# A decode step of a hybrid decoder: the read matrix of the sample state filled by four strided copies in place of sixteen small ones

## Chip, cores and metric

The kernel runs on one core of one Trainium2 chip. The metric is the device time of one launch in microseconds (us), as the median of several runs. What is timed is one inference step for two groups of tokens that share all weights: a prompt of 512 tokens, and a sample group of 8 batches with 4 new tokens each (32 tokens). The kernel holds them side by side as 544 columns; columns 512 to 543 are the sample tokens.

## What is computed

Two layers, each a mixer, a cross-attention into 256 memory tokens, and a feed-forward layer. The mixer of layer 0 joins Mamba-2 state-space heads with sliding-window attention. The change lies in the state-space part of the sample group. For each of 8 batches there is a state of 16 heads by 64 by 128, and the reference does this for the batch's 4 tokens:

```python
def ssd_chunk(h, inp, a_neg):
    x, dt, bm, cm = inp
    rep = SSM_HEADS // SSM_GROUPS
    bh = jnp.repeat(bm, rep, axis=2)
    ch = jnp.repeat(cm, rep, axis=2)
    cs = jnp.cumsum(dt * a_neg, axis=1)
    ...
    scores = jnp.einsum('bthn,bshn->btsh', ch, bh) * decay
    y = jnp.einsum('btsh,bshp->bthp', scores, xdt)
    y = y + jnp.einsum('bthn,bhpn->bthp', ch, h) * jnp.exp(cs)[..., None]
    w_end = jnp.exp(cs[:, -1:, :] - cs)
    h_new = h * jnp.exp(cs[:, -1, :])[:, :, None, None] + jnp.einsum('bsh,bshn,bshp->bhpn', w_end, bh, xdt)
    return h_new, y
```

The matrix that the change fills holds `cm` (C), for the product of C with the old state `h`. There are two groups of 8 heads, each with its own C of 4 columns a batch.

## The kernel before

Nearly all time is matmuls on TensorE (PE), whose 32-bit weights and activations are split into a high and a low part: `wpiece` loads a piece of weights into `room` by the SP queue (L165), ScalarE (ACT) casts the high part (L169) and VectorE (DVE) subtracts to get the low one (L170, tile `split_t`). `mm` (L138) records all matmuls.

The stage around the change is `even`, layer 0. A string of letters there says in which order four generators are advanced: `s` state-space work of the prompt (`ssm`), `p` that of the samples (`ssm_sample`), `f` filler matmuls (the first half of the output projection `wo_e`, then the cross-attention's memory keys and values, `mem_k` and `mem_v`), and `g` the gates with the sum of squares of a norm (`gates`, `norm_tile`, `rstd`). After them comes the second half of `wo_e` (tiles `xh`, `xl`, evacuated by `ssm_evac`). The letters set only where the code stands: the program is built with a scheduler that plays the code through with its own estimates of time and lays down the order of each engine's instructions from that. A small edit can so move instructions of other code.

In `ssm_sample` the tile `CmYi` holds two things. `Cm`, its first 512 columns, is C spread out: for group g and batch b a block of 32 columns in which only columns 4b to 4b+3 are filled, the rest zero (the clear at L971). The 16 copies at L976 on GpSimd (POOL) fill them. A batch's state is loaded into `hb` by SP (L994), two batches to a tile; PE multiplies with `Cm` (matmuls of `hb,CmYi`, all into one PSUM tile, `pi`, here ps_587), POOL decays the state (L1005), PE forms the update from `X4` and `Bm`, DVE adds it (L1006), SP stores it (L1007). When `pi` has its sum over all 8 batches, DVE scales it into `Yi`, the other part of `CmYi` (L1011, one for each group). PE then runs a stretch of small matmuls, here called the small group: 8 of `room,CmYi` (128x32) and 16 of `sE,sxdt` (32x32), into ps_632. DVE adds the result to `xs` (L1019), multiplies by the gates (L913), and forms the parts of the norm's input (`split`, L259).

`mem_v` ends with two evacuations by DVE (L1407, from ps_620 and ps_621). The norm's sum of squares is gathered on POOL (L268), PE adds it over the partitions (`rstd`: ps_645, ps_654), DVE scales it (L302), POOL takes the power (L303), and PE spreads the result over all partitions (ps_646), from where DVE copies it (L310).

Of the kernel before, what the change touches and what calls it, by code (L numbers as in the profile page):

```python
# [106 lines left out]
class Net:  # L107
# [808 lines left out]
    def ssm_sample(self, xs, BC, dt, dtA, sm):  # L916
        B = lambda g: BC[:, g]
        C = lambda g: BC[:, 2 + g]
        nc, I, O = self.nc, self.I, self.O
# [6 lines left out]
        cy = self.H("CmYi")  # L926
        Cm = cy[:, 0:512].rearrange("p (g b t) -> p g b t", g=2, b=8)
# [43 lines left out]
        nc.gpsimd.memset(Cm, 0.0)  # L971
        for g in range(2):
            nc.gpsimd.memset(Yi[64 - 64 * g:128 - 64 * g, 8 * g:8 * g + 8], 0.0)
        for g in range(2):
            for b in range(8):
                nc.gpsimd.tensor_copy(Cm[:, g, b, 4 * b:4 * b + 4], C(g)[:, 512 + 4 * b:516 + 4 * b])  # L976
        yield
        R = sm.tile([32, 16, 32], F32, tag="t2E", bufs=3, name=self.nm("sR"))
        nc.vector.tensor_tensor(R, Ub.unsqueeze(1).to_broadcast([32, 16, 32]), dA.unsqueeze(2).to_broadcast([32, 16, 32]), ALU.mult)
# [37 lines left out]
        for j in range(8):  # L1017
            x = xs[j][:, tok]
# [903 lines left out]
```

## Time and profile before

| what | value |
|---|---|
| median of 3 runs | 1657.58 us (1655.66 to 1658.09) |
| the profiled execution | 1655.56 us |
| its span, first to last instruction | 1653.8 us |
| PE busy | 1623.4 us, 98% of the span |
| DVE, ACT, POOL busy | 1195.5, 795.2, 310.6 us |
| PE's share of the chain that ended last | 73% |
| mean granted TensorE clock | 0.993 of full speed |

The span is the time between the first and the last instruction that the profiler recorded; 1.76 us of the profiled execution lie around it. An engine's busy time is the sum of its instructions. The granted clock is what the chip allowed TensorE: 1.00 is 2.4 GHz, 0.50 is 1.2 GHz, and a value between is a mean over a stretch with both. In a timeline, a row's columns are the start, the time to the end of its last instruction, the engine, line, operation, output from inputs with shape, how many alike stand in the row, and in brackets the idle time of the engine before it with what ended that.

### The profile page before, as it was taken

How to read it: one execution, taken by the hardware profiler on the slowest of the kernel's cores; microseconds unless marked ns; L12 is line 12 of the kernel's file. 1: busy time of each engine (PE TensorE's matmuls, PEld its weight loads, DVE VectorE, ACT ScalarE, POOL GpSimd, SP SyncE). 2: the span in 40 equal slices, each digit the busy share in tenths (PEclk: the TensorE clock that was granted, in tenths of full speed). 3: DMA queues.
4: the chain of work that ended last, by engine and by line, in shares of the span. 5: the costliest groups of instructions: out<-in, count | busy, mean ns of one | idle time of the engine just before them, and what ended most of it. 6: DMA issues, size and time to landing. Idle time of an engine off the chain costs nothing.

```text
span 1653.8 us, 32422 instructions
## 1 busy us (share of the span) xinstructions
PE 1623.4 (98%) x12720; PEld 1518.6 (92%) x12720; DVE 1195.5 (72%) x2327; ACT 795.2 (48%) x1629; POOL 310.6 (19%) x482
## 2 busy tenths in 40 slices
PE   8999999999999999999999999998999999999998
PEld 7999999878998999999999996656989999999997
DVE  6788789888777877777767478546567986767754
ACT  5467545444445444444435266435445444444434
POOL 0022333763322300000002113111313200000002
PEclk9999999999999999999999999999999999999999
DMA  5221334138342232323213433555441322323222
GB/s 194 65 65 52 123 111 161 40 128 290 119 170 73 66 133 87 106 81 111 86 69 138 143 112 119 173 170 178 147 179 54 122 101 77 115 84 103 77 74 84
DMA packets 71221, 189.27 MB, mean 114 GB/s; under 512 B 7612, under 2 KB 34012, under 8 KB 63452
## 3 DMA queue, kind: packets, MB, share of 16 engines
q1 hardware_dynamic: 69932, 185.43, 33.8%
q8 instruction: 100, 1.64, 0.4%
q10 hardware_dynamic: 1056, 1.24, 0.3%
q0 software_dynamic: 80, 0.52, 0.1%
q14 instruction: 53, 0.43, 0.1%
HBM read 172.22 MB, written 14.95 MB: 113 GB/s over the span
## 4 chain that ended last, share of the span: by engine, by line
PE 73%; DVE 2%; ACT 1%; issue 1%; DMA 0%; POOL 0%; POOLq 0%; DVEq 0%; SPq 0%; ACTq 0%
PE ps L138 48%; PE ps L1632 23%; PE ps L141 2%; DMA fr<-wfi 0%; DVE split_t L170 0%; DVE xn L1573 0%; POOL prt L1210 0%; ACT prt L1198 0%; DVE prt L1197 0%; ACT prt L1321 0%; DVE xf L1568 0%; DVE PT L1180 0%; DVE xpr L1473 0%; ACT split_t L169 0%; ACT PT L1180 0%
## 5 line engine op out<-in xcount | busy, mean ns | idle before, releaser
L138 PE MATMUL ps<-xh,split_t 128*128 128x288 f32 (+1 forms) x2304 | 463.2, 293 | 8.2 <-ACT split_t L169 7.8
L138 PEld LDWEIGHTS ps<-xh,split_t 128*128 128x128 f32 x2304 | 371.0, 190 | 11.2 <-ACT split_t L169 7.8
L1632 PE MATMUL ps<-xf,split_t 128*128 128x272 f32 x2592 | 350.5, 289 | 0.2 <-ACT split_t L1605 0.2
L138 PE MATMUL ps<-xl,split_t 128*128 128x256 f32 (+1 forms) x1152 | 337.9, 294 | 0.0
L1632 PEld LDWEIGHTS ps<-xf,split_t 128*128 128x128 f32 x2592 | 335.7, 188 | 1.1 <-DVE split_t L1606 0.8
L268 POOL TENSOR_TENSOR room<-room,sq 128x256 f32<-128x256 f32 (+1 forms) x96 | 84.8, 888 | 782.4 <-ACT sq L267 781.0
L138 PEld LDWEIGHTS ps<-xl,split_t 128*128 128x128 f32 x1152 | 218.6, 190 | 1.1 <-issue 0.4
L138 PE MATMUL ps<-hh,fs 128*128 128x256 f32 (+1 forms) x1024 | 208.3, 288 | 0.0
L169 ACT CAST split_t<-room 128x1024 fp32r<-128x1024 f32 (+1 forms) x128 | 130.3, 1019 | 136.3 <-PE ps L138 108.3
L170 DVE TENSOR_TENSOR split_t<-room,split_t 128x1024 fp32r<-128x1024 f32 (+1 forms) x128 | 163.8, 1282 | 26.9 <-ACT split_t L169 26.1
L1605 ACT CAST split_t<-fr 128x1024 fp32r<-128x1024 f32 x108 | 113.6, 1052 | 113.2 <-PE ps L1632 49.4
L138 PEld LDWEIGHTS ps<-hh,fs 128*128 128x128 f32 x1024 | 165.7, 188 | 0.0
L1606 DVE TENSOR_TENSOR split_t<-fr,split_t 128x1024 fp32r<-128x1024 f32 x108 | 133.0, 1231 | 42.7 <-ACT split_t L1605 40.0
L138 PE MATMUL ps<-hl,fs 128*128 128x256 f32 (+1 forms) x512 | 147.2, 288 | 0.0
L138 PE MATMUL ps<-oh,split_t 128*128 128x288 f32 (+1 forms) x512 | 102.0, 294 | 0.0
L138 PEld LDWEIGHTS ps<-hl,fs 128*128 128x128 f32 x512 | 96.4, 188 | 0.0
L138 PEld LDWEIGHTS ps<-oh,split_t 128*128 128x128 f32 x512 | 81.6, 190 | 1.8 <-issue 1.8
L138 PE MATMUL ps<-ol,split_t 128*128 128x288 f32 (+1 forms) x256 | 75.3, 295 | 0.0
L138 PE MATMUL ps<-hh,split_t 128*128 128x256 f32 (+1 forms) x384 | 73.5, 289 | 0.0
L1606 DVE TENSOR_TENSOR fs<-fr,fs 128x512 fp32r<-128x512 f32 x36 | 24.9, 691 | 65.1 <-ACT fs L1605 65.1
L258 ACT ACTIVATE xh<-x,room 128x256 fp32r<-128x256 f32 (+1 forms) x96 | 48.1, 517 | 48.9 <-DVE x L323 28.6
L1677 ACT CAST fs<-room 128x512 fp32r<-128x512 f32 x64 | 39.7, 620 | 65.0 <-PE ps L138 56.1
(428 smaller groups left out, 3150.2 us busy)
## 6 DMA issues: line engine op xcount, KB each, us to landing
fr<-wfi SPq DMA_DIRECT2D x36, 1024.0 KB
room<-wfo SPq DMA_DIRECT2D x64, 256.0 KB
room<-wo_e SPq DMA_DIRECT2D x16, 512.0 KB
xk<-mem_k SPq DMA_DIRECT2D x8, 1024.0 KB
xv<-mem_v SPq DMA_DIRECT2D x8, 1024.0 KB
room<-wfi SPq DMA_DIRECT2D x16, 512.0 KB
fox_k<-fox_k SPq DMA_DIRECT2D x64, 128.0 KB
fox_v<-fox_v SPq DMA_DIRECT2D x64, 128.0 KB
```

The lines of the kernel that those rows point to most:

```text
L138: return self.placed(self.nc.tensor.matmul(out, lhsT, rhs, start=start, stop=stop))
L141: return self.placed(self.nc.tensor.transpose(out, in_, self.ident[0:k, 0:k]))
L169: nc.scalar.copy(hi[:, 0:n], raw[:, 0:n])
L170: nc.vector.tensor_tensor(lo[:, 0:n], raw[:, 0:n], hi[:, 0:n].bitcast(F32), ALU.subtract)
L258: nc.scalar.activation(hh, src, AF.Copy, scale=g)
L268: nc.gpsimd.tensor_tensor(acc, acc, sq[:, 0:N], ALU.add)
L1605: nc.scalar.copy(hi, t)
L1606: nc.vector.tensor_tensor(lo, t, hi.bitcast(F32), ALU.subtract)
L1632: self.nc.tensor.matmul(ps, w[a][:, k], x[:, b, k], start=start and k == 0 and i == 0, stop=k == 3 and i == 2, skip_group_check=True)
L1677: nc.scalar.copy(hi, raw)
```

## The change

The 16 copies of 4 columns each become 4: for each group one copy of the first seven batches, as 7 blocks of 4 columns that lie 36 apart in `Cm` (L977), and one of the last batch (L978). The same values land in the same places, and the clears stay.

```diff
         for g in range(2):
             nc.gpsimd.memset(Yi[64 - 64 * g:128 - 64 * g, 8 * g:8 * g + 8], 0.0)
+
         for g in range(2):
-            for b in range(8):
-                nc.gpsimd.tensor_copy(Cm[:, g, b, 4 * b:4 * b + 4], C(g)[:, 512 + 4 * b:516 + 4 * b])
+            step = cy[:, 256 * g:256 * g + 252].rearrange("p (b x) -> p b x", x=36)
+            nc.gpsimd.tensor_copy(step[:, :, 0:4], C(g)[:, 512:540].rearrange("p (b t) -> p b t", t=4))
+            nc.gpsimd.tensor_copy(Cm[:, g, 7, 28:32], C(g)[:, 540:544])
```

Lines behind the edit are higher by 2: L1005, L1006, L1011, L1019 and L1407 become L1007, L1008, L1013, L1021 and L1409. No other line of code differs. The scheduler's order does: of PE's 12,087 instructions those from about the 2550th to the 3010th stand in another order, which is the stretch from 343 to 430 us, and the same stretch differs on DVE, ACT, POOL and SP. Ahead of it and behind it the order is the same. In the rows below the first number of a name is the tile's, the second only counts buffers and is lower by 12 in the changed program.

On DVE at the end of `mem_v` the order was, before (`mkv` is what L1407 writes; `CmYi` from `ps_587` is L1011):

```order
L170 TENSOR_TENSOR split_t_68<-room_67,split_t_68 128x1024
L1011 TENSOR_TENSOR CmYi_578_4312<-ps_587_4412,secs_4311 64x512 x2
L1006 TENSOR_TENSOR hb_615_4769<-hb_615_4769,ps_623_4836 128x512
L1006 TENSOR_TENSOR hb_615_4769<-hb_615_4769,ps_624_4840 128x512
L170 TENSOR_TENSOR split_t_68<-room_67,split_t_68 128x1024
L1407 TENSOR_SCALAR mkv_606_4648<-ps_620_4814,room_67 128x512
L259 SCALAR_TENSOR_TENSOR xl_635_4960<-xs_431_2982,room_67,xh_634_4959 128x256 x4
L1407 TENSOR_SCALAR mkv_606_4648<-ps_621_4815,room_67 128x512
```

and is now:

```order
L1008 TENSOR_TENSOR hb_615_4757<-hb_615_4757,ps_618_4767 128x512
L1409 TENSOR_SCALAR mkv_606_4636<-ps_620_4802,room_67 128x512
L170 TENSOR_TENSOR split_t_68<-room_67,split_t_68 128x1024
L1409 TENSOR_SCALAR mkv_606_4636<-ps_621_4803,room_67 128x512
L1013 TENSOR_TENSOR CmYi_578_4312<-ps_587_4400,secs_4311 64x512 x2
L1008 TENSOR_TENSOR hb_615_4757<-hb_615_4757,ps_623_4824 128x512
```

Two evacuations of `mem_v` and a split of weights, which stood behind the two instructions that write `Yi`, stand ahead of them.

On PE, at the same place, the last matmuls of `mem_v` (into ps_620 and ps_621) and what follows up to the small group (`ps_632`) are now:

```order
L138 MATMUL ps_620_4802<-split_t_68,memh_607_4638 128x512
L138 MATMUL ps_621_4803<-split_t_68,memh_607_4638 128x512
L138 MATMUL ps_621_4803<-split_t_68,meml_608_4639 128x512
L138 MATMUL ps_621_4803<-split_t_68,memh_607_4638 128x512
L138 MATMUL ps_587_4400<-hb_625_4863,CmYi_578_4312 32x512 x2
L138 MATMUL ps_623_4824<-X4_4322,Bm_622_4822 128x512
L138 MATMUL ps_624_4828<-X4_4322,Bm_622_4822 128x512
L138 MATMUL ps_660_5079<-xh_634_4947,split_t_68 128x256
L138 MATMUL ps_664_5112<-xh_634_4947,split_t_68 128x256
L138 MATMUL ps_632_4912<-room_67,CmYi_578_4312 128x32
L138 MATMUL ps_632_4912<-sE_586_4396,sxdt_4323 64x32 x2
```

Before, the last four `hb,CmYi` matmuls stood ahead of 24 matmuls of `mem_v` and two of `X4,Bm`, and the small group came behind those; now the last two of them close `mem_v`, with four matmuls between them and the small group.

On DVE at the norm, the rows from the gates to the scaling of the sum (`col` from `ps_645`) were, before:

```order
L259 SCALAR_TENSOR_TENSOR xl_635_4960<-xs_431_2982,room_67,xh_634_4959 128x288 x3
L302 TENSOR_SCALAR col_633_4957<-ps_645_5008 128x2
L259 SCALAR_TENSOR_TENSOR xl_635_4960<-xs_431_2982,room_67,xh_634_4959 128x288
L259 SCALAR_TENSOR_TENSOR xl_640_4984<-xs_448_3259,room_67,xh_639_4983 128x288 x4
L310 COPY room_67<-ps_646_5013 128x256
```

and are now:

```order
L259 SCALAR_TENSOR_TENSOR xl_635_4948<-xs_431_2982,room_67,xh_634_4947 128x288 x3
L259 SCALAR_TENSOR_TENSOR xl_640_4972<-xs_448_3259,room_67,xh_639_4971 128x288 x4
L1008 TENSOR_TENSOR hb_625_4863<-hb_625_4863,ps_631_4905 128x512
L302 TENSOR_SCALAR col_633_4945<-ps_645_4996 128x2
L310 COPY room_67<-ps_646_5001 128x256
```

The scaling has moved behind all eight parts of the norm's input and an update of the state. On PE its reader, ps_646, stood between two `xh` matmuls of the sixth of eight tiles of ps_670; it now stands behind all of ps_670, with the three `128x1` matmuls of ps_654 next. On POOL the seventh L268, for which ps_654 waits, stands behind L303.

## Rows read from the trace of the kernel before

**Rows 1.** The page's busy time by engine, with share of the span and instructions.

```profile
PE 1623.4 (98%) x12720; PEld 1518.6 (92%) x12720; DVE 1195.5 (72%) x2327; ACT 795.2 (48%) x1629; POOL 310.6 (19%) x482
```

**Rows 2.** Instructions on `CmYi`: ns least/median/most, first to last start in us.

```profile
L138 PE MATMUL ps<-hb,CmYi x32: 592/605/617, 360.9 to 390.0; 128*32 128x512 f32 x32
L976 POOL COPY CmYi<-BC x16: 176/178/1176, 336.7 to 345.3; 128x4 f32<-128x4 f32 x16
```

**Rows 3.** Timeline of POOL, 335 to 342 us: around the first nine copies.

```profile
335.49 1.27 POOL L873 TENSOR_TENSOR E<-E,CBm 128x512 f32<-128x512 f32 x1
336.71 0.30 POOL L976 COPY CmYi<-BC 128x4 f32<-128x4 f32 x2
...
340.45 1.90 POOL L976 COPY CmYi<-BC 128x4 f32<-128x4 f32 x7
```

**Rows 4.** Timeline of DVE at the same place.

```profile
336.28 5.30 DVE L170 TENSOR_TENSOR split_t<-room,split_t 128x1024 fp32r<-128x1024 f32 x1 [0.41 <-ACT split_t L169]
```

**Rows 5.** Timeline of PE at the same place.

```profile
342.68 0.66 PE L138 MATMUL ps<-cs,ohs 128*128 128x128 f32 x4 [1.34 <-DVE E L870]
```

**Rows 6.** Stretches: us, busy PE, PEld, DVE, ACT, POOL (instructions), granted clock, DMA share, GB/s.

```profile
345.00:350.00 5.00, 5.00 (x25) 4.43 (x25) 2.22 (x5) 0.29 (x1) 4.33 (x7) 0.68 0.00 0
396.00:400.00 4.00, 4.00 (x32) 3.20 (x30) 3.93 (x8) 2.65 (x5) 0.00 (x0) 0.93 0.69 237
400.00:404.00 4.00, 4.00 (x25) 3.62 (x26) 3.80 (x12) 1.04 (x1) 0.00 (x0) 0.50 0.78 270
404.00:408.00 4.00, 4.00 (x26) 3.96 (x26) 2.88 (x8) 0.13 (x1) 0.00 (x0) 0.72 0.99 354
414.00:420.00 6.00, 5.96 (x44) 5.69 (x45) 5.91 (x10) 1.77 (x4) 4.48 (x5) 1.00 0.65 259
```

**Rows 7.** Timeline of PE, 389 to 403 us: last `hb,CmYi`, end of `mem_v`, small group.

```profile
389.52 1.06 PE L138 MATMUL ps<-hb,CmYi 128*32 128x512 f32 x8
...
396.32 0.39 PE L138 MATMUL ps<-split_t,memh 128*128 128x512 f32 x1
396.55 0.30 PE L138 MATMUL ps<-room,CmYi 128*128 128x32 f32 x2
...
402.94 0.56 PE L138 MATMUL ps<-xh,split_t 128*128 128x256 f32 x1
```

**Rows 8.** Timeline of DVE, 385 to 402 us.

```profile
386.65 1.96 DVE L170 TENSOR_TENSOR split_t<-room,split_t 128x1024 fp32r<-128x1024 f32 x1 [0.67 <-ACT split_t L169]
...
390.76 1.40 DVE L1011 TENSOR_TENSOR CmYi<-ps,secs 64x512 f32<-64x512 f32 x2
...
394.71 1.23 DVE L170 TENSOR_TENSOR split_t<-room,split_t 128x1024 fp32r<-128x1024 f32 x1
396.07 0.75 DVE L1407 TENSOR_SCALAR mkv<-ps,room 128x512 f32<-128x512 f32 x1
...
401.10 0.68 DVE L1006 TENSOR_TENSOR hb<-hb,ps 128x512 f32<-128x512 f32 x1
```

**Rows 9.** Timeline of DVE at the norm, 414 to 418 us.

```profile
414.02 0.16 DVE L302 TENSOR_SCALAR col<-ps 128x2 f32<-128x2 f32 x1 [0.45 <-PE ps L138]
414.09 3.33 DVE L259 SCALAR_TENSOR_TENSOR xl<-xs,room,xh 128x288 fp32r<-128x288 f32 x5
```

**Rows 10.** Timeline of POOL at the norm.

```profile
414.26 0.91 POOL L303 TENSOR_TENSOR col<-col,room 128x2 f32<-128x2 f32 x1 [1.44 <-DVE col L302]
415.14 3.83 POOL L268 TENSOR_TENSOR room<-room,sq 128x288 f32<-128x288 f32 x4
```

**Rows 11.** Timeline of PE at the norm.

```profile
416.05 0.60 PE L138 MATMUL ps<-room,col 128*128 128x128 f32 x4
...
417.48 0.40 PE L138 MATMUL ps<-xl,split_t 128*128 128x288 f32 x1
```

**Rows 12.** Timeline of the SP queue, 376 to 384 us: the issues of loads.

```profile
377.16 0.81 SPq L994 DMA_DIRECT2D hb<-state  x2
...
382.38 0.33 SPq L165 DMA_DIRECT2D room<-wxv  x1
```

## The prediction

> **What bounds the kernel now.** I first read the busy time by engine: PE works 98% of the span [rows 1], so the kernel's time is PE's matmuls plus whatever keeps PE idle or slow. POOL, whose instructions the change cuts, has 19%. A POOL copy can cost time only through who waits for it. So the second view is that of the instructions on `CmYi`: the 16 copies lie between 336.7 and 345.3 us, and the first matmul that reads them starts at 360.9 us [rows 2], over 15 us later. Nobody waits for them. Third come the timelines of POOL, DVE and PE around them [rows 3 to 5], for a hidden cost; there is one, below. Since the scheduler also moved other instructions, the fourth step is the stretch from 389 to 420 us, where the new order differs in ways that PE can feel: stretches [rows 6] and the timelines of PE, DVE and POOL [rows 7 to 11]. The reader is to see there that PE never waits, but that DVE is nearly full (5.91 of 6 us from 414 to 420 us), so what DVE does first decides what PE gets in time.
>
> **The copies themselves: 0.** The sixteen take 16 x 0.18 = 2.9 us at their median, one of them 1.18 [rows 2]. The four new ones were never measured; the bounds are 4 x 0.18 = 0.7 us, if a copy's price hardly depends on its columns, and the old 2.9, if it goes by columns. I take the lower, since the old copies of 4 columns are all fixed cost. The 2 us that POOL saves are covered by the 15 us up to the first reader; were that cover gone, at most 2.2 us of gain would show.
>
> Behind them lies the hidden cost. DVE's L170 at 336.28 us lasts 5.30 us [rows 4], against 1.23 for the same operation at 394.71 [rows 8]. During it POOL works without a break, L873 and copies among it [rows 3], and PE then idles 1.34 us for DVE [rows 5]; shortly after, the clock averages 0.68 over 5 us, a loss of 0.32 x 5 = 1.6 us [rows 6]. But L170 gets through only at the seven copies of 340.45, behind L873, two copies and three more operations of POOL. In the new order the same five operations with the first two new copies stand ahead of that point, so I let the stall stay. By the Trainium skill (SBUF — State Buffer, Who interferes with whom) a DVE instruction with two SBUF inputs and a GpSimd one that reads SBUF contend for one port pair, an exclusive lock that goes to whoever starts first, while the other fully blocks. By that rule L170, waiting since 336.28, should have had the pair when the next POOL instruction ended; the trace agrees with the blocking but has it wait through several of them, and I go by the trace.
>
> **A: a new wait ahead of the small group, +2.1.** Before, `Yi` was written at 390.76 to 392.2 us and the small group that reads it began at 396.55: over 4 us of slack [rows 7, 8]. Now DVE first evacuates ps_620, splits a piece of weights, and evacuates ps_621. Count from the end of the last ps_620 matmul. PE still has three ps_621 matmuls at 0.23 (the step from 396.32 to 396.55), two of `hb,CmYi` (four took 1.0, so 0.5), two `X4,Bm` of the same 512 columns (0.46), and two of 256 columns (0.23): 1.9 us [rows 7]. DVE has 0.75 + 1.23 + 0.75 and the first of two L1013 at 0.70, 3.4 us, or 3.3 with their small overlaps [rows 8]. Least wait: 1.4 us. The split can be held up as at 386.65, where it took 1.96 while POOL ran L1005 [rows 8]: +0.7; the same L1007 of the last state pairs runs here, so I take 2.1. If DVE comes late by an L1008 (0.68) and part of a further split ahead, it is 3.5. Queued behind `Yi` on DVE are the state updates, `xl` parts and L1021; those wait for the small group or have readers after it.
>
> **B: a new wait at the norm, +0.7.** Before, L302 stood amid the L259 parts, POOL's L303 followed at 414.26, and ps_646 ran at 416.05 unwaited, 0.9 us after L303's end [rows 9 to 11]. Now behind the last L259 come L1008 (0.68, about 0.61 to the next start), L302 with 0.24 to L303's start, and L303 (0.91): 1.8 us, of which PE covers 0.3 with the last two ps_670 matmuls. That alone is 1.5. Then ps_654 waits for the seventh L268 (3.83 / 4 = 0.96 us) behind L303, of which ps_646 itself hides some 0.4: 0.5 more, so 2.0 at most [rows 8 to 11]. This counts only if DVE's last L259 and PE's last tile come together, as they did: the part ended at 417.42 and its matmul started at 417.48 [rows 9, 11]. Between L1021 and that point the new order has DVE do a split (1.23) less, so where PE is the late one B shrinks to 0.3 to 1.0. I take 0.7, together with a slower PE under C.
>
> **C: the clock, +1.7.** From 396 to 408 us it falls to 0.50: by means of 0.93, 0.50 and 0.72 [rows 6] at half for 0.56 + 4 + 2.24 = 6.8 us, some 399.4 to 406.2, a loss of 3.4 us. It fell during the small group, which ends at 402.94 [rows 7], and rose 3.3 us after that. In the new order a wait comes ahead of the group and it ends later by the wait, with more of it at half clock, so the low stretch should last longer by about half of its 6.8: 3.4 more at half, a loss of 1.7. Bounds: no longer at all, 0; the group's delay moves it off altogether, -3.4; a second stretch like the one from 345 to 350, 1.6 on top, +3.3.
>
> **The other moves.** The last two state loads on SP stood at 377.16 and now stand behind the fourth `wxv` load, which was issued at 382.38: 5 us later, against 12 us up to the last `hb,CmYi` at 389.5 [rows 7, 12], which itself moves behind `mem_v`, so 0; if that cover goes, PE waits for the load. Stores move behind loads, and nothing on PE reads them. ACT's moved casts and Bm scalings keep their places ahead of their matmuls: 0.
>
> **Sum.** 0 + 2.1 + 0.7 + 1.7 = +4.5 us. The sum stands against the profiled 1655.56 us, so 1660.1; the median of the runs lies 2.0 above that execution, so 1662.1. From the ends, A 1.4 to 3.5, B 0.3 to 2.0, C 0 to 3.3, it is +1.7 to +8.8.
>
> **Rivals.**
> 1. *DVE sets the pace, and the new waits are absorbed.* From 414 to 420 DVE is full, and its last L259 ends 0.06 us before its matmul. With a split fewer in that part DVE gains 1.2 us on PE, while the half-clock stretch runs out at the same time as before and so covers part of A. For it: DVE's 5.91 of 6 us. Against it: before that stretch PE, not DVE, is the late one, and A lies ahead. It decides if PE's arrival at ps_672 is late by less than 1 us. Result: A less 1.2, no C, B at its least, or 2.1 - 1.2 + 0.3 = +1.2: 1658.8, no measurable change.
> 2. *The port opens earlier: not slower, or faster.* If the new wider copy at 336.7 lets L170 in, it ends some 3.6 us earlier, and the 1.34 us of idle PE [rows 5] and the 1.6 of low clock [rows 6] vanish: -2.9. The rule of the page above about the lock points this way. Against it: two copies at 336.71 passed while L170 waited. It decides at the first of the new copies. With A, B and C it leaves +1.6, or 1659.2; with A covered too, -2.9, or 1654.7; with the later half-clock stretch avoided as well (-3.4), 1651.3.
> 3. *Longer stalls.* A 3.5, B 2.0, C 3.3: +8.8, 1666.4. For it: the late L170 at 386.65. Against: all ends at once.
> 4. *The change does nothing but save copies.* Then nobody waits and it is 1657.6. Against: the moved rows on PE and DVE.
>
> **How the numbers follow.** About 0.2%, 3.3 us, is what a measurement of this kernel can tell from no change: below 1654.3 is faster, above 1660.9 slower. The forecast has 0.47, rival 3 0.14, rival 1 0.17, rival 2 0.12 and rival 4 0.07; 0.03 is left for gains in the order that I do not see. The forecast's own range, +1.7 to +8.8, puts about one in ten of its chance below the bound, 0.05 of 0.47. Of rival 2, two thirds end within the bound or below, a third (the waits covered too, and the clock) as faster; with the 0.03 that makes 0.07. So slower 0.42 + 0.14 = 0.56; faster 0.07; same 0.05 + 0.17 + 0.08 + 0.07 = 0.37. The range reaches from rival 2's case with the waits left partly covered, 1655.5, to rival 3's end, 1667.0.
>
> **What would show it.** In the changed profile: four copies on POOL, some 0.7 us in all, unwaited; the long L170 at 336 and PE's 1.3 us idle still there; a wait of PE for DVE `CmYi` at L1013 of about 2 us near 397 us; one for POOL `col` at L303 of 0.3 to 1.5 us near 420; a granted clock of 0.50 that ends later than 406 us. The prediction is wrong if PE shows no wait at either place, if L170 takes under 3 us, or if the time is lost outside 336 to 430 us.

## The result and the profile after

The changed kernel takes 1664.17 us, the median of 7 runs (1660.87 to 1666.00), against 1657.13 for the kernel before, timed beside it (7 runs, 1652.40 to 1658.09). The ratio is 1.0046, 95% interval 1.0032 to 1.0060: **slower by 0.46%, some 7 us**. The profiled execution took 1660.94 us (span 1659.0), the second fastest of its seven, so the lines below show somewhat less than the whole loss. Of all executions in this document one, of run 2, was slow (3170.22 us); the ratios leave it out.

The page's busy time by engine, to be held against [rows 1]:

```profile
PE 1624.8 (98%) x12720; PEld 1520.1 (92%) x12720; DVE 1194.0 (72%) x2327; ACT 795.7 (48%) x1629; POOL 311.1 (19%) x470
```

POOL has twelve instructions fewer and 0.5 us more of busy time; PE's busy time grew by 1.4 us and the rest of the span's growth is PE idling. As before, PE is what counts.

The timeline of POOL and DVE around 336 us (start, duration, engine, line, operation, tiles; in brackets the idle time before and who ended it):

```profile
336.25 0.20 POOL L977 COPY CmYi<-BC 128x28 f32<-128x28 f32 x1
336.39 0.18 POOL L978 COPY CmYi<-BC 128x4 f32<-128x4 f32 x1
...
339.02 1.04 POOL L901 TENSOR_TENSOR hst<-hst,eend 128x512 f32<-128x512 f32 x1
340.00 0.20 POOL L977 COPY CmYi<-BC 128x28 f32<-128x28 f32 x1
340.15 0.18 POOL L978 COPY CmYi<-BC 128x4 f32<-128x4 f32 x1
340.29 1.04 POOL L854 TENSOR_TENSOR xdt<-xdt,wend 128x512 f32<-128x512 f32 x1
344.19 1.28 POOL L873 TENSOR_TENSOR E<-E,CBm 128x512 f32<-128x512 f32 x1 [2.86 <-ACT E L871]
...
335.81 6.60 DVE L170 TENSOR_TENSOR split_t<-room,split_t 128x1024 fp32r<-128x1024 f32 x1 [0.41 <-ACT split_t L169]
```

The four copies are as the prediction took them: 0.76 us in all. A copy of 28 columns takes 0.20 us, one of 4 columns 0.18. But the split L170, waiting since 335.81, took 5.30 us before [rows 4] and takes **6.60** now. It no longer gets through at the copies behind L901 (there the first of seven copies took 1.18 us before [rows 2, 3]); it gets through when POOL has finished L854 and has nothing to do.

All waits of PE in this part of the program that are longer than 0.25 us, from its timeline, but for one at 319.92 us that is the same in both kernels (0.56 here, 0.57 before):

```profile
343.50 1.12 PE L138 MATMUL ps<-cs,ohs 128*128 128x128 f32 x4 [2.64 <-DVE E L870]
...
363.88 1.05 PE L138 MATMUL ps<-hb,CmYi 128*32 128x512 f32 x4 [0.44 <-DMA hb<-state]
...
401.16 0.41 PE L138 MATMUL ps<-room,CmYi 128*128 128x32 f32 x2 [2.62 <-DVE CmYi L1013]
...
423.35 0.71 PE L138 MATMUL ps<-room,col 128*128 128x128 f32 x4 [0.32 <-POOL col L303]
```

The first was 1.34 [rows 5]; the other three are new. L870 stands on DVE behind the long L170. The third is the wait for `Yi`. DVE ahead of it:

```profile
397.19 0.74 DVE L1409 TENSOR_SCALAR mkv<-ps,room 128x512 f32<-128x512 f32 x1
397.85 2.00 DVE L170 TENSOR_TENSOR split_t<-room,split_t 128x1024 fp32r<-128x1024 f32 x1
399.78 0.74 DVE L1409 TENSOR_SCALAR mkv<-ps,room 128x512 f32<-128x512 f32 x1
400.44 1.40 DVE L1013 TENSOR_TENSOR CmYi<-ps,secs 64x512 f32<-64x512 f32 x2
```

This is the sequence of the prediction's step A, with the split held up (2.00 us against 1.23 in [rows 8]) beside POOL's L1007:

```profile
397.73 3.03 POOL L1007 TENSOR_TENSOR hb<-hb,CmYi 128x512 f32<-128x512 f32 x2 [2.37 <-PE ps L138]
```

The first of these two took 1.05 us, the second 2.02: here the split went ahead of the second, although only one large POOL operation followed the hand-over. The 1.96 us at 386.65 [rows 8] came about in the same way, between two L1005.

Stretches (us, busy PE, PEld, DVE, ACT, POOL, then the granted clock):

```profile
343.00:350.00 7.00, 6.50 (x31) 5.65 (x32) 3.71 (x10) 3.15 (x10) 3.08 (x3) 0.54 0.25 75
...
401.00:404.00 3.00, 2.84 (x20) 2.48 (x20) 2.94 (x7) 0.82 (x1) 0.00 (x0) 0.59 0.85 302
404.00:408.00 4.00, 4.00 (x23) 3.14 (x22) 1.87 (x3) 0.00 (x0) 0.00 (x0) 0.50 0.74 242
408.00:412.00 4.00, 4.00 (x19) 3.81 (x19) 3.58 (x14) 0.00 (x0) 0.00 (x0) 0.53 0.84 334
```

Clock 0.50 is the lower of the two levels, 1.2 of 2.4 GHz. Around 345 us it holds for 0.46 x 2 x 7 = 6.4 us of the first row and for some 0.3 us behind it, against 0.32 x 2 x 5 = 3.2 in [rows 6]; the trace's records of the granted clock have 6.8 and 3.4. Around 405 us it holds for 2.5 + 4 + 3.8 = 10.2 us, against the 6.8 of [rows 6].

Counted from the same PE instruction to the same one (at 318 and 430 us before), this part takes 112.0 us before and 118.7 now. Of the 6.74 us, 4.26 are idle time of PE (+1.30, +0.44, +2.62 and +0.32, less two short gaps of 0.41 together that are gone) and the other 2.48 are slower matmuls. The spans differ by 5.2 us; the rest of the program was 1.5 us quicker in this execution than in the one shown of before, at places that the change leaves alone.

### The profile page after: what moved, and what is told of

The parts are those of the page before. It is cut to its first block, busy times and chain, and to the rows that moved or that the text cites. A ratio compares the mean times of both kernels' runs of the same rounds, so it can differ in the third digit from the quotient of the medians.

```text
span 1659.0 us, 32410 instructions
## 1 busy us (share of the span) xinstructions
PE 1624.8 (98%) x12720; PEld 1520.1 (92%) x12720; DVE 1194.0 (72%) x2327; ACT 795.7 (48%) x1629; POOL 311.1 (19%) x470
## 4 chain that ended last, share of the span: by engine, by line
PE 93%; DVE 3%; ACT 2%; issue 1%; POOL 1%; DMA 1%; POOLq 0%; DVEq 0%; ACTq 0%
PE ps L138 67%; PE ps L1634 23%; PE ps L141 3%; DVE split_t L170 1%; DVE xs L913 0%; ACT prt L1200 0%; POOL room L268 0%; ACT split_t L169 0%; ACT xh L258 0%; DMA hb<-state 0%; DMA x<-x 0%; ACT PT L1182 0%; POOL xs L895 0%; DVE prt L1199 0%; ACT prt L1323 0%
## 5 line engine op out<-in xcount | busy, mean ns | idle before, releaser
L268 POOL TENSOR_TENSOR room<-room,sq 128x256 f32<-128x256 f32 (+1 forms) x96 | 85.7, 896 | 780.4 <-ACT sq L267 779.1
L170 DVE TENSOR_TENSOR split_t<-room,split_t 128x1024 fp32r<-128x1024 f32 (+1 forms) x128 | 163.9, 1282 | 27.9 <-ACT split_t L169 27.3
```

Of the source, the lines that this page charges most:

```text
L170: nc.vector.tensor_tensor(lo[:, 0:n], raw[:, 0:n], hi[:, 0:n].bitcast(F32), ALU.subtract)
L268: nc.gpsimd.tensor_tensor(acc, acc, sq[:, 0:N], ALU.add)
```

## The experiments

The ratios are to the kernel before, timed in the same session; where a profile is quoted, it is that of one execution. "The stretch" is the part counted above (112.0 us before, 118.7 changed). In the code cuts, `self.after(i, j)` places instruction i behind j in the scheduler's order, with nothing to wait for, `self.ahead` gives a higher priority, and `...` stands for code left out. By their ratios runs 5, 7 and 8 came out at the time that their theory A named; runs 1 to 4 and 6 did not.

**1. Clears added.** Twelve small clears are added to the changed kernel, so that POOL again has 16 small operations there.

```
 (changed kernel, behind the copies)
+        for i in range(12):
+            nc.gpsimd.memset(Cm[:, i // 6, i % 6, 28:32], 0.0)
```

> The four new copies, and 12 clears of 4 columns that are zero already, so that POOL has 16 small instructions as before; the scheduler then puts the end of mem_v and the norm in the order of before. Theory A (the time was lost by the order: 2.6 us wait for Yi, longer low clock, and the split of 336 us held longer): no wait for CmYi L1013, 0.50 clock no longer than 6.8 us near 400 us, the time within 2 us of before (1655 to 1659). If the clears let the split through as the small copies did, it takes about 5.3 us and PE idles 1.3 us there; if clears, which read nothing, do not, it takes 6.6 and the time is 2 to 3 us above before. Rival B (the strided copies themselves cost the time, in whatever order): the time stays near the changed kernel, 1661 to 1666.

1660.01 us, ratio 1.0020 (1.0006 to 1.0033): more than half of the loss is gone. Timeline of POOL, DVE and PE:

```profile
340.25 1.20 POOL L977 COPY CmYi<-BC 128x28 f32<-128x28 f32 x1
341.39 0.18 POOL L978 COPY CmYi<-BC 128x4 f32<-128x4 f32 x1
341.51 0.22 POOL L980 MEMSET CmYi<- 128x4 f32 x5
...
336.07 5.31 DVE L170 TENSOR_TENSOR split_t<-room,split_t 128x1024 fp32r<-128x1024 f32 x1 [0.42 <-ACT split_t L169]
...
361.86 1.05 PE L138 MATMUL ps<-hb,CmYi 128*32 128x512 f32 x4 [1.19 <-DMA hb<-state]
```

The split is back at 5.31 us, let in at the very copy of 28 columns that it passed by in the changed kernel; the wait for L1013 is gone. Five clears stand behind the two copies there, so operations that only write count in the train too, and neither the copy's width nor its strides keep the split out. What is left over goes with a third order of the instructions, which has waits of its own (1.19 us for a state load); the stretch takes 115.2 us.

**2. The four copies behind the last L854.** This takes them out of the train that the split waits behind.

```
 (changed kernel; x854 is the last L854)
             ...
+            self.after(i, self.x854)
```

> The four new copies held behind POOL's L854, so that no copy stands in POOL's train from 335 to 341 us; the scheduler's order near 390 to 420 us is again that of before (Yi ahead of both mem_v evacuations). Theory A: no wait at L1013; the split waits for the end of L854, some 6 us long, PE idles about 2 us there and the clock is low for 6.8 us: about 2 to 3 us above before, 1659 to 1660. Rival C (copies in the train are what holds the split up, not the train): the split takes under 4 us, PE's idle time of 1.3 us goes, the time is at or under before, 1654 to 1657.

1661.94 us, ratio 1.0033 (1.0022 to 1.0045). From the timelines of POOL and DVE:

```profile
341.07 1.20 POOL L977 COPY CmYi<-BC 128x28 f32<-128x28 f32 x1
...
336.14 6.07 DVE L170 TENSOR_TENSOR split_t<-room,split_t 128x1024 fp32r<-128x1024 f32 x1 [0.41 <-ACT split_t L169]
```

L170 takes 6.07 us and gets in at the first copy behind L854, which takes 1.20; PE idles 2.11 us. The wait for L1013 is not there, since the order behind moved once more. The stretch takes 117.3 us, with 0.81 us of waiting for `memh` among it. That the split goes through where the copies stand is shown; a gain is not.

**3. `Yi` first.** The changed kernel with the two `Yi` instructions (L1013) given a higher priority.

```
 (changed kernel; m1 = self.mark() at the start of the same function)
+        with self.ahead(m1):
             ...
                 nc.vector.tensor_tensor(Yi[a, 8 * g:8 * g + 8], pi[a].rearrange(...
```

> The changed kernel with the two instructions that write Yi given priority: they stand ahead of the second mem_v evacuation, but still behind the first and behind the split. Theory A: PE's wait for L1013 falls by that evacuation, from 2.6 to about 1.9 us, the low clock stays at 10 us, the time is 0.5 to 1 us under the changed kernel, 1663. Rival D (the wait is given back at the norm, where DVE sets the pace): no change, 1664, with a longer wait at L303 in place of it.

1664.52 us, ratio 1.0050 (1.0036 to 1.0065): no gain. From the timelines of PE and DVE:

```profile
400.61 0.50 PE L138 MATMUL ps<-X,Bm 128*128 128x512 f32 x1 [2.42 <-DVE hb L1009]
...
403.00 0.64 PE L138 MATMUL ps<-room,CmYi 128*128 128x32 f32 x2 [1.66 <-DVE CmYi L1015]
...
398.21 1.75 DVE L170 TENSOR_TENSOR split_t<-room,split_t 128x1024 fp32r<-128x1024 f32 x1 [2.96 <-ACT split_t L169]
```

The single wait became two of 4.1 us together. In this order a split stands ahead of what PE waits for, and its weights come late: ACT, which casts them at 397.13, stood idle 8.82 us until a load of `wo_e` landed, and DVE 2.96 us until that cast was done. So the edit moved more than `Yi`, and what the wait for `Yi` is worth can't be read from this run.

**4. The split behind the four L870.** The long L170 is tied behind L870, so that PE's `E` comes without it.

```
 (changed kernel; late for piece 6 of wo_e alone, relu is the last L870)
         ...
+        if late:
+            self.after(i, self.relu)
```

> The changed kernel with the split of 336 us placed behind the four L870 on DVE, for which PE waits at 343 us; the order at L1013 stays. Theory A: PE's idle time of 2.6 us near 343 us goes, with it the low clock there or most of it (3.4 us), while the wait for L1013 stays at 2 to 3 us: 4 to 6 us under the changed kernel, 1658 to 1660. Rival E (what waits behind the split is late anyway, or the wait moves to the matmuls that need the split): less than 1.5 us under the changed kernel, with an idle time of PE for split_t near 351 us.

1666.98 us, ratio 1.0061 (1.0045 to 1.0078): the slowest of all. From the timelines of DVE and PE:

```profile
338.22 6.15 DVE L170 TENSOR_TENSOR split_t<-room,split_t 128x1024 fp32r<-128x1024 f32 x1
...
344.42 0.51 PE L138 MATMUL ps<-oh,split_t 128*128 128x256 f32 x2 [3.11 <-DVE split_t L170]
...
367.70 0.39 PE L138 MATMUL ps<-meml,split_t 128*128 128x256 f32 x1 [1.80 <-DVE meml L261]
```

The split is held up for 6.15 us all the same, only later, and now PE waits for the split itself, besides 2.24 us for `Yi`. Moving the split out of the way of L870 moves PE's wait on to the split's own reader; nothing is gained.

**5. The new copies in the old order.** The changed kernel with twelve idle copies ahead of the four. The instructions of every engine then stand in the order of the kernel before, but for one matmul that slid by a place, with the four strided copies last of the sixteen.

```
 (changed kernel, ahead of the copies)
+        for i in range(12):
+            nc.gpsimd.tensor_copy(Cm[:, i // 6, i % 6, 28:32], Cm[:, i // 6, i % 6, 24:28])
```

> The four new copies with 12 more copies of 4 zero columns onto 4 zero columns of the same tile ahead of them, so that POOL has its 16 small copies again; every engine's order is that of before, but for which small copy is which. Theory A (time lost by the order and by how long the split is held): the same as before within 1.5 us, the split of 336 us at 5.3 us, PE idle 1.3 us there, no wait at L1013. Rival B (the strided copies themselves cost the time): 4 us or more above before.

1654.09 us, ratio 0.9996 (0.9985 to 1.0007): the time of before. From the timelines of POOL and DVE, then two stretches:

```profile
340.15 1.91 POOL L976 COPY CmYi<-CmYi 128x4 f32<-128x4 f32 x7
...
335.99 5.30 DVE L170 TENSOR_TENSOR split_t<-room,split_t 128x1024 fp32r<-128x1024 f32 x1 [0.41 <-ACT split_t L169]
```

```profile
401.00:404.00 3.00, 3.00 (x22) 2.96 (x23) 3.00 (x12) 0.99 (x1) 0.00 (x0) 0.71 0.77 209
404.00:408.00 4.00, 4.00 (x27) 3.86 (x27) 4.00 (x11) 1.52 (x4) 0.00 (x0) 0.79 1.02 392
```

L170 takes 5.30 us and PE idles 1.33, both as before, and there is no wait for `Yi`. **The strided copies cost nothing; the order that came with them does.** One thing differs from the profile of before, with the same order: near 400 us the clock is low for 1.7 + 1.7 = 3.4 us in place of 6.8, and the stretch takes 110.8 us in place of 112.0. So one profile of an order does not fix the length of that low stretch.

**6. The wait for `Yi` alone.** The kernel before, with its `Yi` instructions behind both evacuations of `mem_v`, where the change has them.

```
 (kernel before; mve is the last evacuation of mem_v, L1407)
             ...
+            self.after(i, self.mve)
```

> The kernel before, with nothing else but Yi (L1011) put behind both mem_v evacuations, as in the changed order; the 16 small copies stay. Theory A: Yi is written at about 399.8 to 400.5 us instead of 390.8, so PE waits some 3 to 3.5 us ahead of the small group, and the low clock near 400 us lasts 10.2 us instead of 6.8 (1.7 more): 3 to 5 us above before, 1660 to 1661. Rival F (the wait falls into low clock and is hidden, DVE sets the pace after it): under 1.5 us above before.

1657.21 us, ratio 1.0010 (1.0000 to 1.0019). From the timeline of PE, then a stretch of its table:

```profile
397.04 0.39 PE L138 MATMUL ps<-xl,split_t 128*128 128x256 f32 x1 [0.25 <-DVE xl L259]
...
399.48 0.41 PE L138 MATMUL ps<-room,CmYi 128*128 128x32 f32 x2 [0.52 <-DVE CmYi L1011]
```

```profile
408.00:412.00 4.00, 4.00 (x21) 4.00 (x21) 4.00 (x10) 3.37 (x9) 1.59 (x2) 0.50 0.94 296
```

PE waits 0.77 us, not 2.6, because in this order no split stands between the two evacuations, and the scheduler put matmuls on `xh` and `xl` ahead of the small group on PE. But the low clock holds to 412 us, as in the changed kernel, and for 10.2 us in all, against 6.8 in the profile of before and 3.4 in run 5. So in this execution the later small group drew out the half-clock stretch even though the wait was short. Of the loss of 0.46%, this order by itself gives 0.1%.

**7. The long split alone.** The kernel before, with 14 of its 16 copies behind the last L854.

```
 (kernel before)
                 ...
+                if 8 * g + b > 1:
+                    self.after(i, self.x854)
```

> The kernel before, with 14 of the 16 small copies held behind POOL's L854: the first two stay at 336.7 us. Behind L901 then follows L854 at once, as nearly in the changed kernel; Yi stays ahead of the evacuations. Theory A (the split gets in when a small copy follows L901, and else only behind L854): the split takes 6.1 to 6.6 us, PE idles 2.1 to 2.6 us and the clock there is low for 6.8 us: 2 to 3 us above before. Rival G (the split's length is a matter of the moment and not of the copies): 5.3 us as before, the time within 1 us of before.

1656.88 us, ratio 1.0015 (1.0003 to 1.0027). From the timelines of POOL and DVE:

```profile
340.25 1.04 POOL L854 TENSOR_TENSOR xdt<-xdt,wend 128x512 f32<-128x512 f32 x1
341.24 2.27 POOL L976 COPY CmYi<-BC 128x4 f32<-128x4 f32 x10
...
336.08 6.30 DVE L170 TENSOR_TENSOR split_t<-room,split_t 128x1024 fp32r<-128x1024 f32 x1 [0.41 <-ACT split_t L169]
```

With the copies gone from behind L901 the split gets in one operation later, PE idles 2.33 us and the clock there is low for 6.8 us. By the ratio that costs 0.15%, 2.5 us, though the medians (1656.88 and 1655.72) are only 1.2 us apart, and it does not stand quite alone (some of PE's and DVE's instructions slid a little, with a wait of 0.37 us for `memh`). Runs 9 to 11 give the cost more closely. It is **the term that the prediction had at nothing**.

**8. The change once more**, in the session of runs 5 to 7.

> The changed kernel again, to be set beside the others on this chip and to see how its two waits vary. Theory A: 5 to 8 us above before; the split again at 6.6 us with 2.6 us of idle PE, the wait at L1013 again 2 to 2.6 us. Rival G (a matter of the moment): a split of 5.3 us or another length this time.

1662.72 us, ratio 1.0044 (1.0029 to 1.0060). L170 takes 6.60 us again, PE waits 2.64 us for L870, and 3.10 for `Yi`:

```profile
402.05 0.64 PE L138 MATMUL ps<-room,CmYi 128*128 128x32 f32 x2 [3.10 <-DVE CmYi L1013]
```

The two losses repeat; the second varies by half a microsecond, and the half-clock stretch behind it lasted 13.7 us here in place of 10.2. This is part of why the execution shown above lost less than the median. At the norm PE does not wait for `col` here, where it waited 0.32 us in the first profile.

**9 to 11. How many copies let the split in.** Three versions of the kernel before, the order of DVE kept and that of PE but for a few matmuls, with two, three or four of the 16 copies between L901 and L854 and the rest behind L854.

```
 (kernel before; 3, 4 or 5 in place of n)
                 ...
+                if 8 * g + b > n:
+                    self.after(i, self.x854)
```

> The kernel before with its order on every engine kept, but of the 16 old copies only two stand ahead of L895, two between L901 and L854, and twelve behind L854 (eight at once, then four as before). The question is why the split L170 at 336 gets through 1.3 us later in the changed kernel. Theory N (the train decides: the waiting split gets through at a hand-over only where POOL's next short operations are more than two in a row, and the two of the changed kernel are too few): it stays out behind L901 as in the changed kernel and gets in behind L854, so L170 takes 6.5 to 6.7 us, one of the copies behind L854 takes 1.2, and PE idles 2.5 to 2.7. Rival K (the kind decides: the old copies of 4 columns let it in, the new one of 28 does not): L170 5.3, the first copy behind L901 takes 1.2, PE idles 1.3. Rival M (seven in a row are needed) expects what N does.

> As the run with two copies between L901 and L854, but with three there and eleven behind L854. Theory N (more than two short operations in a row): L170 gets in behind L901, 5.3 us, the first of the three copies takes 1.2, PE idles 1.3. Rival M (a longer train is needed): L170 6.6 to 6.9, in behind L854, PE idles 2.6 to 2.9. Rival K (the kind of copy): 5.3, as with two.

> As the two runs ahead of it, with four copies between L901 and L854 and ten behind L854. Theory N: L170 5.3 us, PE idles 1.3. Rival M (seven in a row): L170 6.8 to 7.0 in behind L854, PE idles 2.8 to 3.0. If three let it stay out and four let it in, the threshold lies between.

One execution each: 1659.09, 1654.60 and 1654.43 us, beside a median of 1654.45 for the kernel before. A single time can't tell such differences apart; the timelines can. With two:

```profile
339.44 0.30 POOL L976 COPY CmYi<-BC 128x4 f32<-128x4 f32 x2
...
340.69 2.03 POOL L976 COPY CmYi<-BC 128x4 f32<-128x4 f32 x8
...
335.26 6.56 DVE L170 TENSOR_TENSOR split_t<-room,split_t 128x1024 fp32r<-128x1024 f32 x1 [0.41 <-ACT split_t L169]
```

With three:

```profile
339.72 0.42 POOL L976 COPY CmYi<-BC 128x4 f32<-128x4 f32 x3
...
335.54 6.68 DVE L170 TENSOR_TENSOR split_t<-room,split_t 128x1024 fp32r<-128x1024 f32 x1 [0.41 <-ACT split_t L169]
```

With four:

```profile
340.26 1.55 POOL L976 COPY CmYi<-BC 128x4 f32<-128x4 f32 x4
...
336.10 5.30 DVE L170 TENSOR_TENSOR split_t<-room,split_t 128x1024 fp32r<-128x1024 f32 x1 [0.41 <-ACT split_t L169]
```

Two and three small copies run through at their usual price and the split stays out; of four, one is held up by 1 us and the split is in. So at this hand-over the threshold lies between three and four, not above two as the first theory had it, and not at seven. The kind of copy does not decide: old ones of 4 columns stay closed too when they are only two or three. Whether POOL's count or the length of the train in time (0.42 us against about 0.55) decides was not tried. Nor is it a rule for every hand-over: between two L1007 the split got in without any train (2.00 us, in the profile after), and so it did in run 4 at 364.39 us (2.07 us). What tells these places apart is open.

The stretch gives the price of the long split, with PE's order all but kept: 113.3 us in each of the two runs where it stays out (9 and 10), 110.7 in run 11 and 110.8 in run 5, where it gets in early. That is 2.5 us, the same within 0.1 us in both pairs.

**12. The same train early.** The kernel before with six copies ahead of L895, where two stood.

```
 (kernel before; m1 is the mark at the start of the same function)
+                with self.ahead(m1, 3000) if 8 * g + b < 6 else ExitStack(): nc.gpsimd.tensor_copy(...
```

> The kernel before, with six of the 16 copies given a higher priority, so that all six stand ahead of L895 at 336.7 us, where two stood, three between L901 and L854 and seven behind it; further on the scheduler moves other instructions too. Theory N (a train of more than two short operations lets the waiting split in, wherever it stands): L170 gets in at the first of the six, 1.5 to 2.5 us in all in place of 5.3, that copy takes 1.2 to 1.3, L870 starts before 339, PE's wait for L870 (1.34 before) is under 0.5 and the clock there stays at full: by this 2 to 3 us below before, if the moved instructions behind it cost nothing. Rival P (the place decides: the hand-over behind L873 never opens): L170 as before, 5.3 us or more by the four further copies, PE idles 1.3 or more, time of before or above.

1658.67 us, ratio 1.0026 (1.0014 to 1.0039). From the timelines of POOL, DVE and PE, then a stretch:

```profile
336.14 1.82 POOL L976 COPY CmYi<-BC 128x4 f32<-128x4 f32 x6
...
335.71 1.60 DVE L170 TENSOR_TENSOR split_t<-room,split_t 128x1024 fp32r<-128x1024 f32 x1 [0.41 <-ACT split_t L169]
337.23 1.11 DVE L870 TENSOR_SCALAR E<-ps,ncs 128x128 f32<-128x128 f32 x4
...
360.21 0.95 PE L138 MATMUL ps<-memh,split_t 128*128 128x256 f32 x3 [1.49 <-ACT memh L258]
363.55 0.58 PE L138 MATMUL ps<-meml,split_t 128*128 128x256 f32 x1 [0.52 <-DVE meml L259]
```

```profile
345.00:350.00 5.00, 5.00 (x44) 3.95 (x42) 5.00 (x4) 1.67 (x3) 3.40 (x3) 1.00 0.01 3
```

What was expected of the split came true: it takes 1.60 us in place of 5.30, PE no longer waits for L870, and the granted clock from 345 to 350 us is 1.00 in place of 0.68 [rows 6]. So a train lets the split in at this earlier hand-over too. The time did not follow: the higher priority moved other instructions, and PE waits for `memh` and `meml`. The low clock has only moved, too: it now holds from 360.3 to 367.1 us, for 6.8 us. The median is 0.26% above before; where the whole of that goes was not followed up. No version was found that beats the kernel before.

## Why the prediction was right, and where it was wrong

It said slower, 1662.1 us in a range of 1655.5 to 1667.0; measured were 1664.17 and 1662.72. Against the 1657.58 that it started from it forecast +4.5; beside its own runs of before the change measured +7.0. Term by term, in us:

| term | forecast | measured in the profile after | in the second run of it |
|---|---|---|---|
| the copies | 0 | 0 (0.76 of POOL, nobody waits; run 5) | 0 |
| the long L170 | 0 (stays) | idle +1.30; 3.4 longer at half | the same |
| state loads | 0 | idle +0.44 | +0.34 |
| A, wait for `Yi` | +2.1 | +2.62 | +3.10 |
| C, clock at 405, against the profile of before | 3.4 longer at half | 3.4 longer | 6.8 longer |
| the same, against runs 5 and 9 to 11 | | 6.8 longer | 10.2 longer |
| B, norm | +0.7 | +0.32 | 0 |

**Copies: right.** Four copies take 0.76 us, the lower bound, and run 5 shows that they leave the time alone. Rival 4, that only this happens, fell because the moved order matters.

**The long split: the step that failed.** "I let the stall stay" took the place of the hand-over as given, with the same operations ahead of it. The runs showed that at this place what comes behind the hand-over decides: the split got in at four or more small operations, or when POOL was idle. The change leaves two there, so the split waits for one more L854, 1.04 us and a bit. This cost 1.3 us of idle PE and twice the stretch at half clock. Run 7 gives the whole as 0.15% (0.03 to 0.27), 2.5 us with a wide interval, and the stretches of runs 5 and 9 to 11 give the same 2.5 us: about the difference between forecast and result. The page that the prediction weighed, the Trainium skill (SBUF — State Buffer, Who interferes with whom), has the waiting engine blocked, and the trace agrees (5.30 and 6.60 us in place of 1.23); that whoever starts first has the lock does not tell where a waiting split comes in here, which runs 9 to 12 show for this place.

**Rival 2** had the port open at the new wide copy. It fell in the changed kernel, where only two small operations stand there; with six (run 12) the split does get in there.

**A: right in place and mechanism, a little small.** 2.62 and 3.10 against 2.1, inside its 1.4 to 3.5. The split between the two evacuations was held up as supposed (2.00 us). Run 6 adds what the prediction did not see: with `Yi` just as far back, but no split between the evacuations and other PE work ahead of the group, the wait is 0.77 us and the loss 0.1%.

**C: right in mechanism, its size partly luck.** Against the one profile of before, the half-clock stretch near 400 us grew by the forecast 3.4 us. But the 6.8 us that the prediction started from are not what this order always gives: runs 5 and 9 to 11, which have it, show 3.4 us each, and the second run of the change has 13.7. So the stretch grew by 3.4 to 10.2 us, according to which executions are set side by side. Both low stretches together, at 345 and at 405 us, grew by 6.8 us in the first profile, which at half speed would be 3.4 us; the slower matmuls amount to 2.5, some of what PE does there not taking twice as long. In run 6 part of the small group ran at either level: from one pair of `room,CmYi` matmuls to the next it took 0.57 us (400.05 to 400.62) at the upper one and 0.92 (402.69 to 403.61) at the lower, which is 1.6 times as long.

**B: too high.** PE waits 0.32 us in the first profile, the low end of what was given for the case that PE is late, and not at all in the second. So the 0.7 was too high, and nothing like its 2.0 showed.

**State loads: a cover that was not looked at.** The prediction spoke of the last two loads; the load that came late is of the first six. Their first issue moved from 356.78 to 359.25 us on SP's queue, and the first `hb,CmYi` matmul waits 0.44 us for it. This is what the prediction named for a lost cover, at another load.

**Rival 1** (DVE's full time absorbs the waits) fell: PE's waits show up in the time. **Rival 3**, +8.8, had the right size nearly, but for another reason: its waits A and B stayed below its ends, and the split, which it left alone, made up for it.

By whole times a part of the sum stays open: run 7 (0.15%) and run 6 (0.10%) together give 0.25% of the 0.45%, and run 6 holds a wait of 0.77 us in place of 2.6 to 3.1. The stretch closes more of it. It takes 118.7 us in the first profile of the change, 5.5 more than in runs 9 and 10, which have the long split but otherwise the order of before. Of the 5.5, 3.0 are idle time of PE (the waits for `Yi`, the state load and the norm, less the two short gaps); the other 2.5 are slower matmuls, with 6.8 us more of low clock near 400 us. This compares single executions, and in the second run of the change the stretch takes 120.0 us.

## What to carry to other kernels

An edit that saves time on an engine nobody waits for may still move a scheduler's whole order; count what the new order does to the engine that sets the time before counting what the edit saves. Where a DVE instruction held up by POOL gets in can depend on what stands next on POOL: before thinning out a train of small POOL operations, look whether a stalled DVE instruction gets through there. And where a wait goes in ahead of a group of small matmuls, price the clock behind it with the wait, from more than one profile.

## What the runs showed of the hardware

- Around 336 us a DVE split waiting for POOL let up to nine POOL operations start ahead of it (6.68 us, run 10) and got in only at a train of four or more small ones, or when POOL had nothing to do; with two or three it stayed out. The first operation of the train then takes 1.2 us in place of 0.2. Elsewhere the same split got in between two large POOL operations (L1007 at 397.73 us in the changed kernel, the second 2.02 us in place of 1.05), so the train is no general condition.
- A strided POOL copy of 128x28 takes 0.20 us, one of 128x4 takes 0.18: seven times the columns cost 0.02 us more. A 128x4 clear amid others took 0.09 us (run 1).
- The half-clock stretch near 400 us lasted 3.4 us (runs 5, 7 and 9 to 11) or 6.8 (before) where PE went into the small matmul group without a wait, and 10.2 (the change, run 6) or 13.7 (run 8) with a wait of 0.5 to 3.1 us just ahead of it.
